# Delta rule: the small merge matmuls of a head as single items of the planner, and its last merge in two batches of five chunks side by side

## The chip, the cores and the metric

The kernel runs on one core of one Trainium2 chip. The time is device microseconds of one execution. TensorE (PE in the profile; PEld is its weight load), VectorE (DVE), ScalarE (ACT), GpSimd (POOL) and SyncE (SP) each work through their own instructions in order, and wait for one another through semaphores. Transfers are issued by SyncE, some by ScalarE.

## What is computed

One layer over 1024 latent and 256 context tokens of width 1024. Branch A is a gated delta rule in two directions, 8 heads of 128 by 128; branch B is a differential attention. The part that matters here, cut from the reference:

```python
    decay = jnp.where(incl, jnp.exp(jnp.where(incl, gc[..., :, None] - gc[..., None, :], 0.0)), 0.0)
    a_mat = jnp.where(strict, jnp.einsum('nbhid,nbhjd->nbhij', kc * bc[..., None], kc) * decay, 0.0)
    eye = jnp.eye(CHUNK, dtype=a_mat.dtype)
    t_mat = lax.linalg.triangular_solve(eye + a_mat, jnp.broadcast_to(eye, a_mat.shape),
                                        left_side=True, lower=True)
    u = t_mat @ (vc * bc[..., None])
    w = t_mat @ (kc * (bc * jnp.exp(gc))[..., None])
...
        v_new = u_i - jnp.einsum('bhck,bhkv->bhcv', w_i, s)
        s_next = s * jnp.exp(gl_i)[..., None, None] + jnp.einsum('bhck,bhcv->bhkv', kd_i, v_new)
```

`t_mat` is the inverse of a lower triangular matrix for every head, direction and chunk. The kernel takes chunks of 128 tokens, ten of them (NT): eight of the latents and two of the context.

## The kernel before

**Preparing a head (`gdn_prep`, from L972).** For each head, X holds ten chunks times two directions of 128x128. It is filled with the broadcast sums of the gates (gcd, on SyncE, L980), turned into decay factors on ScalarE (L997, L999), and multiplied with the Gram matrices (gram) that TensorE makes. The 32x32 diagonal blocks go through memory to VectorE, which inverts them in 31 steps (tmp, ts, L1048 and L1050). They come back as RR (R and its transpose Rt), and TensorE merges them:

- first merge, 32x32: pz = (block below the diagonal) x (inverse); VectorE negates it into Z (L1071); p2 = inverse x Z is the missing 32x32 block, p3 the same in the transposed order for t64. Forty pz, forty p2 and twenty p3 matmuls for a head (4, 4 and 2 for a chunk). ScalarE and VectorE copy them to X (L1087, L1089) and t64.
- last merge, 64x64: pz6 and Z6 (L1110), then pu6, two matmuls for a chunk in each. GpSimd clears a quarter of X (L1119), ScalarE copies pu6 into X (L1121, L1122), scales X by beta (L1126), and SyncE stores it to xd (L1129). This is done for chunks 5 to 9, and then for chunks 0 to 4.

In the profile pz and pz6 are both "pz", p2 and p3 are "p", pu6 is "pu"; they stand at L55, the helper `mm`. The 32x32 and 64x64 matmuls use quarters and halves of TensorE's array, several beside each other.

**The scan (`scan`, L1183; `out_chunk`).** Two streams, one for each direction, go through the ten chunks of a head: three chained 128x128 float32 matmuls (chain) with VectorE (r, S) and ScalarE (vd, vn) between, and two more for the output (out). It reads X back from xd (x, L1176) and keys, values and queries (sk, kk, vv, sq, L1161).

**The fill.** Input projections that nothing else here needs (mm, 128x512, operands of 128x128) are used as fill: they may go wherever TensorE has a hole.

**What sets the order.** All of this stage is written in an order that a planner (`flow`, `step`) makes when the program is built. Each piece of work is a generator, and each `yield` is one item: the engine, its assumed time, the items that it waits for, the code to emit, and for some TensorE items the share of the array that they keep warm. At every step the planner takes the item that can start first, with a bias for each stream (scan 0, preparation 3) and the fill last. The engines' real order is then fixed. One small matmul was one item of 0.03 us (32x32) or 0.065 us (64x64), so items of other streams could be placed between two of them.

**PSUM.** Merges, gram, the output transposes (oT) and the key transposes (tr) share two buffers (`self.banks`, `yield self.psum(n)` waits for n of them). pz takes one, p2 and p3 take two, and pz6 and pu6 took one each.

A head's X buffer is used again two heads later: the reload X<-gcd waits until both stores to xd have landed.

After the stage comes the attention (S, t, v), ordered by the same planner with other rules (`turn_flow`), the merge of the branches, and the output projection.

Of the kernel before, what the change touches and what calls it, by code (L numbers as in the profile page):

```python
# [23 lines left out]
NT = LT // P  # L24
# [10 lines left out]
PE, DVE, ACT, POOL, DMA, ADMA, DV2, PL1 = range(8)  # L35
# [8 lines left out]
class Block:  # L44
# [8 lines left out]

    def mm(self, out, lhsT, rhs, start=True, stop=True):
        self.nc.tensor.matmul(out, lhsT, rhs, start=start, stop=stop)  # L55

    def tr(self, out, src):
        self.nc.tensor.transpose(out, src, self.ident[:src.shape[0], :src.shape[0]])  # L58
# [913 lines left out]
    def gdn_prep(self, h):  # L972
        nc, PT, V = self.nc, self.gt_, self.nc.vector
        T = lambda nm, shape, tag=None: self.g1.tile(shape, F32, tag=tag or nm, name=nm)
        G = lambda nm, shape: self.gh[h % 2].tile(shape, F32, tag=nm, name=nm)
        X = G("X", [P, 2, NT, P])
# [18 lines left out]
        for d in range(2):  # L995
            for c in range(NT):
                t = yield ACT, 0.293, [ld[d]], lambda: nc.scalar.activation(  # L997
                    X[:, d, c], X[:, d, c], AF.Abs, bias=self.gcc[:, c, d * H + h:d * H + h + 1], scale=-1.0)
# [31 lines left out]
        B = lambda b: slice(32 * b, 32 * b + 32)  # L1030
# [66 lines left out]

        lo, hi = slice(0, 64), slice(64, 128)
        Z6 = T("Z6", [P, NT, 64], "w4")
        ends = []  # L1100
        for c0, nb in ((5, 5), (0, 5)):
            cs = slice(c0, c0 + nb)
            yield self.psum()
            b = self.banks.pop(0)
            pz = PT("pz6")[:, :nb * 64].rearrange("p (c f) -> p c f", f=64)
            for j in range(nb):
                c = c0 + j
                t = yield PE, 0.065, [tx, b], lambda: self.mm(pz[lo, j], X[hi, 0, c, lo], X[hi, 0, c, hi]), 0.5
                t = yield PE, 0.065, [tx, b], lambda: self.mm(pz[hi, j], X[lo, 1, c, hi], X[lo, 1, c, lo]), 0.5
            tz = yield DVE, 0.398, [t], lambda: V.tensor_scalar_mul(Z6[:, cs], pz, -1.0)  # L1110
            self.banks.append(tz)
            yield self.psum()
            b = self.banks.pop(0)
            pu = PT("pu6")[:, :nb * 64].rearrange("p (c f) -> p c f", f=64)
            for j in range(nb):
                c = c0 + j
                t = yield PE, 0.065, [tz, t6, b], lambda: self.mm(pu[lo, j], t64[lo, c], Z6[lo, c]), 0.5
                t = yield PE, 0.065, [tz, t6, b], lambda: self.mm(pu[hi, j], t64[hi, c], Z6[hi, c]), 0.5
            e = [(yield PL1, 0.38, [tz], lambda: nc.gpsimd.memset(X[hi, 0, cs, lo], 0.0)),  # L1119
                 (yield PL1, 0.38, [tz], lambda: nc.gpsimd.memset(X[lo, 1, cs, hi], 0.0))]  # L1120
            f = [(yield ACT, 0.43, [t], lambda: nc.scalar.copy(X[lo, 0, cs, hi], pu[lo])),  # L1121
                 (yield ACT, 0.43, [t], lambda: nc.scalar.copy(X[hi, 1, cs, lo], pu[hi]))]  # L1122
            self.banks.append(f)
            for d in range(2):
                for c in range(c0, c0 + nb):
                    t = yield ACT, 0.263, [e, f], lambda: nc.scalar.activation(  # L1126
                        X[:, d, c], X[:, d, c], AF.Copy, scale=self.beta[:, c, d * H + h:d * H + h + 1])
                ends.append(t)
            self.store_t.setdefault(h, []).append((yield DMA, 2.2, ends, lambda: nc.sync.dma_start(  # L1129
                self.xd[h][:, :, cs], X[:, :, cs])))  # L1130
        self.merge = self.stored = h + 1
# [732 lines left out]
```

## Time and profile before

| | us |
|---|---|
| median of 3 runs | 2091.38 |
| lowest and highest | 2090.12, 2092.27 |
| span of the profiled execution (first to last instruction) | 2084.9 |
| first and last merge matmul (pz of head 0, pu of head 7) | 632.2, 1303.1 |
| first and last scan matmul (chain) | 803.9, 1366.1 |
| TensorE busy, 600 to 1400 us | 778.7 of 800 |

For the profiled execution the profile gives the span, which leaves out what lies before the first and after the last instruction; the median is 6.5 us longer. In the rows of the timeline a start, a length, the engine, the line, the operation and the tiles follow each other; xN is the number of records. Matmuls overlap in the array, so the distance from one start to the next is what a matmul costs, and the length is not.

### The profile page before, as it was taken

To read this page: it belongs to the slowest core of one execution; us is meant where nothing else is said; L and a number is where in the kernel's file an instruction comes from. 1 tells how busy PE (TensorE), PEld (TensorE's weight loads), DVE (VectorE), ACT (ScalarE), POOL (GpSimd) and SP (SyncE) were. 2 spreads that over 40 slices of the span, in tenths; PEclk is the share of its full clock that TensorE was granted. 3 is DMA by queue.
4 is the path that set the end of the run, shared out by engine and by line. 5 is a ranking of instruction groups with operands and counts; after the bars stand their busy time and mean duration, and the time that the engine had idled before them with its cause. 6 is when DMAs were issued, how large, how long until landed. Compare 5 with 4: busy or idle time off the path is not lost.

```text
span 2084.9 us, 38611 instructions
## 1 busy us (share of the span) xinstructions
PE 1985.0 (95%) x14207; PEld 1733.2 (83%) x14207; DVE 1424.1 (68%) x3582; ACT 1070.7 (51%) x2328; POOL 774.7 (37%) x644
## 2 busy tenths in 40 slices
PE   8999898899999999999999999999899999999999
PEld 3888677789999997888778888887777878887899
DVE  4897668867876895657646885237767979874532
ACT  4344344444235453566456655448667878873210
POOL 1213224204441431323333232326555656764122
PEclk9999999999999999999999999999999999998999
DMA  9446567555446456656765763857465655236452
GB/s 310 124 139 152 150 143 190 139 166 172 138 136 214 134 200 174 222 179 207 195 214 151 252 199 109 252 161 213 115 175 134 174 158 148 87 126 207 149 157 90
DMA packets 395840, 352.24 MB, mean 169 GB/s; under 512 B 145423, under 2 KB 344689, under 8 KB 395651
## 3 DMA queue, kind: packets, MB, share of 16 engines
q1 hardware_dynamic: 345443, 302.58, 49.4%
q10 hardware_dynamic: 50208, 47.19, 7.5%
q8 instruction: 112, 1.84, 0.4%
q14 instruction: 77, 0.63, 0.1%
HBM read 232.63 MB, written 117.08 MB: 168 GB/s over the span
## 4 chain that ended last, share of the span: by engine, by line
PE 54%; DMA 9%; DVE 7%; ACT 4%; issue 2%; SPq 1%; POOL 1%; ACTq 0%; DVEq 0%; POOLq 0%
PE mm L55 22%; PE chain L55 5%; PE s L55 4%; PE mo L55 4%; PE v L55 4%; PE m L55 3%; PE ma L55 3%; PE out L55 3%; DVE S L1453 2%; PE t L58 2%; DMA wq<-in_w_oa_dram 2%; ACT S L1466 1%; DMA hx<-in_w_in_dram 1%; DMA qh<-qd 1%; PE gram L55 1%
## 5 line engine op out<-in xcount | busy, mean ns | idle before, releaser
L55 PE MATMUL mm<-hs,wh 128*128 128x512 f32 x1024 | 358.1, 414 | 0.0
L414 PE MATMUL mm<-hs,wh 128*128 128x512 f32 (+1 forms) x1024 | 291.5, 371 | 18.4 <-ACT xc L454 18.4
L55 PE MATMUL mm<-wh,hs 128*128 128x256 f32 x1472 | 273.3, 285 | 0.0
L1453 DVE TENSOR_SCALAR_CACHE_REDUCE S<-s,rsq 128x512 f32<-128x512 f32 (+1 forms) x384 | 242.4, 656 | 30.6 <-PE s L55 28.2
L414 PEld LDWEIGHTS mm<-hs,wh 128*128 128x128 f32 x1024 | 187.9, 194 | 52.5 <-ACT xc L454 21.7
L55 PEld LDWEIGHTS mm<-wh,hs 128*128 128x128 f32 x1472 | 230.9, 192 | 0.4
L1490 POOL TENSOR_TENSOR S<-S 128x1280 f32<-128x1280 f32 x64 | 188.9, 2954 | 100.0 <-ACT S L1483 91.1
L55 PE MATMUL mm<-hs,wl 128*128 128x512 f32 x512 | 213.7, 417 | 1.0 <-POOL wl L766 1.0
L55 PEld LDWEIGHTS mm<-hs,wh 128*128 128x128 f32 x1024 | 189.3, 191 | 27.1
L55 PE MATMUL mm<-wl,hs 128*128 128x256 f32 x736 | 210.3, 286 | 0.0
L1466 ACT ACTIVATE S<-S,mn 128x1280 f32<-128x1280 f32 x128 | 174.7, 1366 | 36.0 <-DVE mn L1465 35.5
L414 PE MATMUL mm<-hs,wl 128*128 128x512 f32 (+1 forms) x512 | 189.0, 369 | 0.0
L459 DVE SCALAR_TENSOR_TENSOR ac<-xc,smallT,ac 128x1284 f32<-128x1284 f32 (+1 forms) x96 | 159.0, 1656 | 14.2 <-ACT ac L455 11.9
L55 PE MATMUL s<-kk,qh 128*128 128x512 f32 (+1 forms) x384 | 146.7, 383 | 7.5 <-DVE S L1453 7.3
L55 PEld LDWEIGHTS mm<-wl,hs 128*128 128x128 f32 x736 | 141.1, 192 | 0.3
L55 PE MATMUL s<-kk,ql 128*128 128x512 f32 (+1 forms) x384 | 136.1, 364 | 0.1
L1527 DVE TENSOR_TENSOR al<-t,ah 128x512 fp32r<-128x512 f32 (+1 forms) x192 | 107.7, 595 | 13.2 <-ACT ah L1522 12.8
L414 PEld LDWEIGHTS mm<-hs,wl 128*128 128x128 f32 x512 | 99.2, 194 | 15.3
L55 PEld LDWEIGHTS mm<-hs,wl 128*128 128x128 f32 x512 | 97.7, 191 | 14.4 <-POOL wl L766 1.1
L1522 ACT CAST ah<-t 128x512 fp32r<-128x512 f32 (+1 forms) x192 | 90.3, 515 | 25.5 <-PE t L58 24.0
L1048 DVE TENSOR_TENSOR tmp<-ab,ts 80x31 f32<-80x31 f32 (+15 forms) x248 | 97.6, 394 | 8.1 <-DMA ab<-da 2.7
L58 PE MATMUL t<-ct,S 128*128 128x128 f32 x640 | 97.4, 278 | 5.3 <-DVE al L1527 4.8
(291 smaller groups left out, 5048.1 us busy)
## 6 DMA issues: line engine op xcount, KB each, us to landing
hx<-in_w_in_dram ACTq DMA_DIRECT2D x64, 256.0 KB
wr<-in_w_in_dram SPq DMA_DIRECT2D x30, 512.0 KB
X<-gcd SPq DMA_DIRECT2D x16, 640.0 KB
kd<-col SPq DMA_DIRECT2D x40, 256.0 KB
xd<-X SPq DMA_DIRECT2D x16, 640.0 KB
x<-xd SPq DMA_DIRECT2D x80, 128.0 KB
kk<-kd SPq DMA_DIRECT2D x32, 320.0 KB
wr<-in_w_in_dram ACTq DMA_DIRECT2D x18, 512.0 KB
```

What stands on the lines that cost most here:

```text
L55: self.nc.tensor.matmul(out, lhsT, rhs, start=start, stop=stop)
L58: self.nc.tensor.transpose(out, src, self.ident[:src.shape[0], :src.shape[0]])
L414: nc.tensor.matmul(pt[:, :n], wt[:, k, cs], ht[:, k, o:o + n], start=i == 0, stop=i == 3 * KT - 1)
L459: nc.vector.scalar_tensor_tensor(ac[:, w], xc[:, o + j:o + j + wd // parts], self.convw(j, ct), ac[:, w], ALU.mult, ALU.add)
L1048: t = yield DV2, n * w / 960.0 + 0.08, [t, t1], lambda: V.tensor_tensor(tv, ab[:, j + 1:, j:j + 1].to_broadcast([80, n, w]), ts[:, j, :w]. ...
L1453: e = yield DVE, 0.675 if m == 512 else 0.408, [e, self.sfree[c].get(n - 4 + c)], lambda: self.nc.vector.tensor_scalar(x["S"][c][:, o:o + ...
L1466: x["x"].append((yield ACT, 1.36, [e], lambda: nc.scalar.activation(S, S, AF.Exp, bias=x["mn"][:, c:c + 1], scale=-1.0, accum_out=w["l0"][ ...
L1490: e = yield POOL, 2.9, [e], lambda: self.nc.gpsimd.tensor_tensor(S0, S0, S1, ALU.add)
L1522: e = yield ACT, 0.48 if nb == 4 else 0.27, [t, y["old", k]], lambda: self.nc.scalar.copy(y["ah", k][:, :, q], pv)
L1527: t = yield DVE, 0.603 if k < 2 else 0.322, [e, y["old", k]], lambda: self.nc.vector.tensor_tensor(y["al", k][:, :, q], pv, y["ah", k][:, ...
```

## The change

The 40 pz of a head are one item, so are its 40 p2, and its 20 p3, through the new helper `mms`, which emits a list of matmuls. In p2 and p3 the order was four p2, two p3 for each chunk in turn; now all p2 come ahead of all p3. The last merge takes both halves together: 20 pz6 in one item into two PSUM buffers, two negations, 20 pu6 in one item into two buffers, and then for each half what followed before (clear, copy, scale, store). The assumed time of an item is the sum or a little more: 1.2, 1.2, 0.4, 1.3 and 1.3 us.

```diff
+    def mms(self, ops):
+        for x in ops:
+            self.mm(*x)
...
-        for c in range(NT):
-            for (b1, b2) in ((0, 1), (2, 3)):
-                t = yield PE, 0.03, [tt, b], lambda: self.mm(pz[B(b1), c], X[B(b2), 0, c, B(b1)], Rt[B(b2), c]), 0.25
-                t = yield PE, 0.03, [tt, b], lambda: self.mm(pz[B(b2), c], X[B(b1), 1, c, B(b2)], R[B(b1), NT + c]), 0.25
+        t = yield PE, 1.2, [tt, b], lambda: self.mms(
+            x for c in range(NT) for b1, b2 in ((0, 1), (2, 3)) for x in (
+                (pz[B(b1), c], X[B(b2), 0, c, B(b1)], Rt[B(b2), c]), (pz[B(b2), c], X[B(b1), 1, c, B(b2)], R[B(b1), NT + c]))), 0.25
...
-        for c in range(NT):
-            for (b1, b2) in ((0, 1), (2, 3)):
-                t = yield PE, 0.03, [tz, b], lambda: self.mm(p2[B(b1), c], R[B(b1), c], Z[B(b1), c]), 0.25
-                t = yield PE, 0.03, [tz, b], lambda: self.mm(p2[B(b2), c], Rt[B(b2), NT + c], Z[B(b2), c]), 0.25
-            t3 = yield PE, 0.02, [tz, b], lambda: self.mm(p3[B(1), c], Z[B(0), c], R[B(0), c]), 0.25
-            t3 = yield PE, 0.02, [tz, b], lambda: self.mm(p3[B(2), c], Z[B(3), c], Rt[B(3), NT + c]), 0.25
+        t = yield PE, 1.2, [tz, b], lambda: self.mms(
+            x for c in range(NT) for b1, b2 in ((0, 1), (2, 3)) for x in (
+                (p2[B(b1), c], R[B(b1), c], Z[B(b1), c]), (p2[B(b2), c], Rt[B(b2), NT + c], Z[B(b2), c]))), 0.25
+        t3 = yield PE, 0.4, [tz, b], lambda: self.mms(
+            x for c in range(NT) for x in ((p3[B(1), c], Z[B(0), c], R[B(0), c]), (p3[B(2), c], Z[B(3), c], Rt[B(3), NT + c]))), 0.25
...
-        for c0, nb in ((5, 5), (0, 5)):
-            cs = slice(c0, c0 + nb)
-            yield self.psum()
-            b = self.banks.pop(0)
-            pz = PT("pz6")[:, :nb * 64].rearrange("p (c f) -> p c f", f=64)
-            for j in range(nb):
-                c = c0 + j
-                t = yield PE, 0.065, [tx, b], lambda: self.mm(pz[lo, j], X[hi, 0, c, lo], X[hi, 0, c, hi]), 0.5
-                t = yield PE, 0.065, [tx, b], lambda: self.mm(pz[hi, j], X[lo, 1, c, hi], X[lo, 1, c, lo]), 0.5
-            tz = yield DVE, 0.398, [t], lambda: V.tensor_scalar_mul(Z6[:, cs], pz, -1.0)
-            self.banks.append(tz)
-            yield self.psum()
-            b = self.banks.pop(0)
...
-                t = yield PE, 0.065, [tz, t6, b], lambda: self.mm(pu[lo, j], t64[lo, c], Z6[lo, c]), 0.5
-                t = yield PE, 0.065, [tz, t6, b], lambda: self.mm(pu[hi, j], t64[hi, c], Z6[hi, c]), 0.5
...
+        halves = slice(5, 10), slice(0, 5)
+        v6 = lambda nm: PT(nm)[:, :5 * 64].rearrange("p (c f) -> p c f", f=64)
+        yield self.psum(2)
+        b = [self.banks.pop(0), self.banks.pop(0)]
+        pz = [v6("pz6"), v6("pz6")]
+        t = yield PE, 1.3, [tx, b], lambda: self.mms(
+            x for cs, z in zip(halves, pz) for j in range(5) for c in (cs.start + j,) for x in (
+                (z[lo, j], X[hi, 0, c, lo], X[hi, 0, c, hi]), (z[hi, j], X[lo, 1, c, hi], X[lo, 1, c, lo]))), 0.5
+        tz = []
+        for cs, z in zip(halves, pz):
+            tz += [(yield DVE, 0.398, [t], lambda: V.tensor_scalar_mul(Z6[:, cs], z, -1.0))]
+            self.banks.append(tz[-1])
+        yield self.psum(2)
+        b = [self.banks.pop(0), self.banks.pop(0)]
+        pu = [v6("pu6"), v6("pu6")]
+        t = yield PE, 1.3, [tz, t6, b], lambda: self.mms(
+            x for cs, u in zip(halves, pu) for j in range(5) for c in (cs.start + j,) for x in (
+                (u[lo, j], t64[lo, c], Z6[lo, c]), (u[hi, j], t64[hi, c], Z6[hi, c]))), 0.5
+        for cs, u in zip(halves, pu):
...
```

More of the change, by code (lines that the diff above doesn't have):

```diff
@@ L1099, in gdn_prep @@
         Z6 = T("Z6", [P, NT, 64], "w4")
-        ends = []
-        for c0, nb in ((5, 5), (0, 5)):
-            cs = slice(c0, c0 + nb)
-            yield self.psum()
-            b = self.banks.pop(0)
-            pz = PT("pz6")[:, :nb * 64].rearrange("p (c f) -> p c f", f=64)
-            for j in range(nb):
-                c = c0 + j
-                t = yield PE, 0.065, [tx, b], lambda: self.mm(pz[lo, j], X[hi, 0, c, lo], X[hi, 0, c, hi]), 0.5
-                t = yield PE, 0.065, [tx, b], lambda: self.mm(pz[hi, j], X[lo, 1, c, hi], X[lo, 1, c, lo]), 0.5
-            tz = yield DVE, 0.398, [t], lambda: V.tensor_scalar_mul(Z6[:, cs], pz, -1.0)
-            self.banks.append(tz)
-            yield self.psum()
-            b = self.banks.pop(0)
-            pu = PT("pu6")[:, :nb * 64].rearrange("p (c f) -> p c f", f=64)
-            for j in range(nb):
-                c = c0 + j
-                t = yield PE, 0.065, [tz, t6, b], lambda: self.mm(pu[lo, j], t64[lo, c], Z6[lo, c]), 0.5
-                t = yield PE, 0.065, [tz, t6, b], lambda: self.mm(pu[hi, j], t64[hi, c], Z6[hi, c]), 0.5
[L1119 to L1122, printed above, removed]
@@ L1123, in gdn_prep @@
+        for cs, u in zip(halves, pu):
+            e = [(yield PL1, 0.38, tz, lambda: nc.gpsimd.memset(X[hi, 0, cs, lo], 0.0)),
+                 (yield PL1, 0.38, tz, lambda: nc.gpsimd.memset(X[lo, 1, cs, hi], 0.0))]
+            f = [(yield ACT, 0.43, [t], lambda: nc.scalar.copy(X[lo, 0, cs, hi], u[lo])),
+                 (yield ACT, 0.43, [t], lambda: nc.scalar.copy(X[hi, 1, cs, lo], u[hi]))]
             self.banks.append(f)
+            ends = []
             for d in range(2):
-                for c in range(c0, c0 + nb):
-                    t = yield ACT, 0.263, [e, f], lambda: nc.scalar.activation(
+                for c in range(cs.start, cs.stop):
+                    t1 = yield ACT, 0.263, [e, f], lambda: nc.scalar.activation(
```

2 lines of the change are left out of this document (1 added, 1 removed).

## The prediction

> **What bounds the kernel now.** I read the page first (span, busy shares, the 40 slices, the shares of the chain), then busy time by stage, then TensorE's waits, then the timeline at single merges.
>
> ```profile
> span 2084.9 us, 38611 instructions
> ...
> PE 1985.0 (95%) x14207; PEld 1733.2 (83%) x14207; DVE 1424.1 (68%) x3582; ACT 1070.7 (51%) x2328; POOL 774.7 (37%) x644
> ...
> PE 54%; DMA 9%; DVE 7%; ACT 4%; issue 2%; SPq 1%; POOL 1%; ACTq 0%; DVEq 0%; POOLq 0%
> ```
>
> TensorE is busy for 95% of the span, and it has 54% of the chain that ended last. The merges lie between 632 and 1303 us. By stages (busy time of each engine, granted clock, DMA share and rate):
>
> ```profile
> 600.00:800.00 200.00, 198.57 (x2061) 192.71 (x2061) 159.21 (x417) 90.26 (x205) 55.76 (x47) 1.00 0.59 185
> 800.00:1000.00 200.00, 191.23 (x1603) 162.57 (x1602) 125.99 (x381) 118.43 (x352) 62.09 (x87) 0.98 0.63 197
> 1000.00:1200.00 200.00, 189.87 (x1549) 160.74 (x1548) 127.10 (x360) 115.74 (x316) 62.20 (x78) 0.97 0.65 200
> 1200.00:1400.00 200.00, 198.99 (x1594) 169.30 (x1593) 97.73 (x260) 99.05 (x292) 63.87 (x83) 1.00 0.59 177
> ```
>
> In these 800 us TensorE is idle for 1.4 + 8.8 + 10.1 + 1.0 = 21.3 us only; no other engine reaches 80% in any of the four. The projection matmuls (mm) fill every hole that the scan leaves. They still have work when the scan is over: the chain, in order of time, holds this piece after the last scan step at 1366 us:
>
> ```profile
> 1367.73 13.41 PE mm L55 x59
> ```
>
> So the end of this stage is set by the sum of what TensorE does plus its waits. Its waits here (total, times, longest):
>
> ```profile
> PE chain L55 <- ACT vd L1214: 7.9, 3, 4.7
> PE chain L55 <- DMA x<-xd: 2.9, 1, 2.9
> PE oT L58 <- POOL oa L1283: 2.6, 1, 2.6
> PE chain L55 <- DMA hx<-in_w_in_dram: 2.0, 1, 2.0
> ```
>
> None of them is on a merge. A merge is worth something here only through TensorE's own time, or through waits that it makes elsewhere.
>
> **The change part by part.** (1) *Units.* The planner now places each merge step as one item, so no other matmul can come between its small ones. How often did that happen? I counted, in the instruction order of the two programs, unbroken runs of 32x32 and of 64x64 matmuls on TensorE. Before: 62 runs of 32x32 and 49 of 64x64. After: 21 and 16. The number of small matmuls is the same (800 and 320), as is that of all others. So 41 + 33 = 74 breaks go, 58 of which are due to the units and 16 to the joined halves of the last merge. Heads 0 and 1 had no broken 32x32 run before; the breaks are in heads 2 to 7, where the scan runs beside the merges.
>
> What is a break worth? The timeline has a whole run (start, length, x records; a float32 matmul leaves two records):
>
> ```profile
> 631.96 0.28 PE L55 MATMUL mm<-wh,hs 128*128 128x256 f32 x1
> 632.17 0.89 PE L55 MATMUL pz<-RR,X 32*32 32x32 f32 x80
> 632.98 0.39 PE L55 MATMUL mm<-wh,hs 128*128 128x256 f32 x1
> ```
>
> And a broken one, followed by a place where the same kind of scan matmul stands among its like:
>
> ```profile
> 827.37 0.52 PE L55 MATMUL pz<-RR,X 32*32 32x32 f32 x36
> 827.82 0.49 PE L55 MATMUL out<-S,sq 128*128 128x128 f32 x2
> 828.24 0.25 PE L55 MATMUL pz<-RR,X 32*32 32x32 f32 x4
> 828.42 0.49 PE L55 MATMUL chain<-r,x 128*128 128x128 f32 x2
> ...
> 837.17 0.39 PE L55 MATMUL chain<-vd,kk 128*128 128x128 f32 x2
> 837.39 0.39 PE L55 MATMUL out<-vn,qk 128*128 128x128 f32 x2
> ```
>
> From start to next start (lengths overlap, so they can't be added): 36 records take 827.82 - 827.37 = 0.45 us, 4 records take 0.18. That is 0.0084 a record and a fixed 0.146 for each run. The whole run of 80 agrees: 0.146 + 80 x 0.0084 = 0.82, against 0.81 measured. The scan matmul between two runs takes 0.42, against 0.22 in a row of its like: 0.20 more. A 32x32 break therefore costs 0.146 + 0.20 = **0.35 us**. For 64x64:
>
> ```profile
> 848.91 0.57 PE L55 MATMUL pu<-Z,t 64*64 64x64 f32 x12
> 849.40 0.49 PE L55 MATMUL out<-S,sq 128*128 128x128 f32 x2
> 849.82 0.45 PE L55 MATMUL pu<-Z,t 64*64 64x64 f32 x8
> 850.20 0.50 PE L55 MATMUL mm<-hs,wl 128*128 128x512 f32 x1
> ```
>
> 12 records take 0.49, 8 take 0.38: 0.0275 a record and 0.16 fixed; with the 0.20 of the matmul between them (0.42 again), **0.36 us**. The sum: 41 x 0.35 + 33 x 0.36 = 14.4 + 11.9 = **26.2 us** of TensorE time. Nothing hides it, since the engine has next to no idle time there; it is lost only if TensorE then waits.
>
> (2) *The order inside p2 and p3.* Forty p2 then twenty p3 instead of four and two by turns: the same records in the same array form, at nothing; bounds 0 and one fixed 0.35 a head where other work falls between the two units (five heads; already in the count of runs).
>
> (3) *The last merge in two batches.* Both halves' pz6 in one go of 40 records (0.16 + 40 x 0.0275 = 1.3 us), then two DVE scalings, then both pu6. It needs both PSUM buffers at once, twice a head; before it needed one at a time. Who else wants them (gram, oT, tr) is put elsewhere in the fixed order, so this shows as waits, not as work. The scan's matmuls, which could slip in before, stand behind up to 1.3 us of small matmuls; the fills cover that as they covered the rest.
>
> (4) *The stores.* Still two a head, but in SyncE's order they now stand side by side for heads 4 to 6, and for heads 4 and 5 the reload X<-gcd comes right behind, ahead of sk, kk and vv of the next scan; before, for head 4, these stood between the stores. This is the dangerous part. Before, at head 4 (second store, reload, ScalarE's first use of it, and the scan matmul that waited for ScalarE):
>
> ```profile
> 1066.57 0.53 SPq L1129 DMA_DIRECT2D xd<-X  x1
> ...
> 1073.18 0.85 SPq L980 DMA_DIRECT2D X<-gcd  x2
> ```
>
> ```profile
> 1085.64 3.04 ACT L997 ACTIVATE X<-X,gcc 128x128 f32<-128x128 f32 x10 [5.96 <-DMA qk<-qkd]
> ...
> 1089.21 1.28 ACT L999 ACT_TABLE_LOAD   x1
> ```
>
> ```profile
> 1093.99 1.22 PE L55 MATMUL chain<-vd,kk 128*128 128x128 f32 x4 [4.69 <-ACT vd L1214]
> ```
>
> The reload was issued 6.6 us after the store and used 12.5 us later; ScalarE works in order, so vd of the scan stood behind it, and TensorE stood still for 4.7 us. Then the clock fell, as it did after other waits:
>
> ```profile
> 1002.00:1006.00 4.00, 1.99 (x12) 1.43 (x11) 0.05 (x1) 1.10 (x3) 1.63 (x1) 1.00 1.07 356
> 1006.00:1010.00 4.00, 4.00 (x17) 3.37 (x15) 0.58 (x2) 1.15 (x3) 0.00 (x0) 0.57 0.69 141
> ...
> 1091.00:1098.00 7.00, 4.01 (x25) 3.19 (x25) 1.79 (x5) 6.12 (x14) 2.17 (x3) 0.53 0.01 2
> ```
>
> A wait of 2.0 us cost a further 4 x 0.43 = 1.7 us at half clock; that of 4.7 us a further 7 x 0.47 = 3.3 us, 8.0 in all.
>
> The Trainium skill ("TensorE: Matmul & The Clock Gate", the table under "Why this matters for your kernels") asks for no idle gaps over about 3 us, since one idle window takes the clock to half. Here the measurement is stricter: 2.0 us was enough. By the page's limit the two waits that I add below would cost 3.4 us less, for a sum of -18.7.
>
> (5) *ScalarE.* Its order holds two more activation table loads than before, at 1.28 us: 2.6 us. At 51% busy they may cost nothing; the upper end is that both fall ahead of a vd, 2.6. I take 2.6, as vd is the longest wait above.
>
> (6) *Everything behind.* The planner's clocks change, so the order of all engines differs until deep in the attention stage (some 1,400 of 4,000 TensorE places moved); the work is the same. Its cost is unknown in sign: no row of before shows it. I bound it by one wait of the largest kind, 8.0 us either way, and take 0.
>
> What TensorE saves, it partly returns by arriving early. From nothing to all 26.2; I take two waits of the sizes that this stage shows for late transfers (2.9 and 2.0), each with 1.7 us of half clock: 8.3 us.
>
> Sum: -26.2 + 8.3 + 2.6 = **-15.3 us**. The profiled span of 2084.9 becomes 2069.6. The median of the runs, 2091.4, lies 6.5 above the span; carried over, **2076 us**.
>
> **The rivals.** *All of it arrives* (22%): 26.2 us, 2084.9 - 26.2 + 6.5 = 2065. For it: TensorE is 97% busy in the stage, and fills are left after the scan. Against: the 21.3 us of idle show that the fixed order is often a few us off.
>
> *The waits eat it* (15%): three waits like that at 1094, 24.0 us, leave 2.2: 2089. For it: DMA runs at 177 to 200 GB/s in the stage, and the stores come in pairs now.
>
> *Slower by the reload* (10%): SyncE stands at X<-gcd until the second of two stores has landed, and the next scan's loads stand behind it. The issues of 600 to 1400 us hold it for six heads, two each:
>
> ```profile
> X<-gcd SPq DMA_DIRECT2D x12, 640.0 KB
> ```
>
> If each head gives a wait of 8.0 us where one did, 5 x 8.0 = 40.0 are added: 2084.9 - 26.2 + 40.0 + 6.5 = 2105. It decides from four new waits on (26.2 / 8.0 = 3.3). Against: heads 2, 3 and 7 keep other issues between, and the planner starts the scan later where it expects the loads late.
>
> *The clock* (2%): long runs of small matmuls leave most of the array empty. If each of the 16 stretches of merges brought 1.7 us of half clock, 27 us would go: 2092. Against it, the whole 32x32 runs of head 0 before:
>
> ```profile
> 632.00:637.00 5.00, 4.61 (x220) 4.16 (x219) 4.66 (x14) 0.42 (x1) 1.50 (x4) 1.00 0.02 3
> ```
>
> The clock there is 1.00. *Doing nothing* isn't open: the runs are shorter in number in the program itself.
>
> **How the numbers follow.** Forecast 45%, and 6% for an attention order that is worse or better by more than 8 us. Less than 0.2%, 4.2 us, can't be told from no change. The forecast, the full gain, half of the eaten one and some of the rest are faster: 0.78; within 0.2%: 0.11; slower: 0.11. The range goes from the full gain with one wait of 3.7 less (2062) to the eaten case (2090); beyond lie the reload and the clock above, and two lucky waits below.
>
> **What would show it.** Right: 37 runs of small matmuls in the timeline, each with about 0.15 us fixed, and the stretch from the first merge to the last projection matmul shorter by about the sum. Returned waits: idle in 600 to 1400 over 21 us, with chain as the waiter and vd, x<-xd or X<-gcd as the cause. Reload: waits of 4 to 5 us at several heads, with clock rows near 0.5 behind them. Wrong would be: a merge stage no shorter though the runs are whole and the idle time is the same (then a break costs no 0.35), or a gain lost behind 1400 us, in the attention's waits.

## The result, and the profile after

The changed kernel takes **2106.9 us** (median of 4 runs, 2105.5 to 2108.3), the kernel before beside it 2090.8 (4 runs, 2089.7 to 2092.3). The ratio is **1.0075, interval 1.0061 to 1.0089**: 16 us slower, where 15 us faster was forecast. The time lies outside the range.

From the page of the changed kernel, the span and the busy times:

```profile
span 2106.0 us, 38576 instructions
...
PE 1972.6 (94%) x14207; PEld 1731.6 (82%) x14207; DVE 1416.7 (67%) x3582; ACT 1072.3 (51%) x2330; POOL 777.1 (37%) x644
```

TensorE is busy for 1972.6 us against 1985.0, 12 us less, and the span is 21 us longer all the same. So there are some 33 us more of idle time. By stages of the changed kernel (the same columns as before: busy time of PE, PEld, DVE, ACT, POOL, then clock, DMA share, GB/s):

```profile
600.00:800.00 200.00, 194.28 (x2057) 190.06 (x2056) 157.56 (x398) 90.43 (x207) 56.92 (x48) 1.00 0.55 173
800.00:1000.00 200.00, 191.67 (x1618) 166.26 (x1616) 122.97 (x373) 118.49 (x334) 60.85 (x82) 0.98 0.64 202
1000.00:1200.00 200.00, 181.94 (x1597) 155.97 (x1597) 127.51 (x375) 115.98 (x324) 61.00 (x80) 0.95 0.66 204
1200.00:1400.00 200.00, 192.81 (x1534) 167.91 (x1533) 99.55 (x271) 98.50 (x304) 68.45 (x87) 0.98 0.55 171
1400.00:1900.00 500.00, 459.89 (x2870) 398.11 (x2870) 384.79 (x1301) 362.26 (x598) 295.81 (x146) 0.96 0.55 148
```

And the last of these stretches, mostly attention, in the kernel before:

```profile
1400.00:1900.00 500.00, 470.26 (x2926) 406.63 (x2925) 390.54 (x1301) 365.50 (x604) 305.01 (x154) 0.97 0.55 154
```

From 600 to 1400 us TensorE is now idle for 5.7 + 8.3 + 18.1 + 7.2 = 39.3 us, before for 21.3. From 1400 to 1900 it is idle for 40.1, before for 29.7. The waits of TensorE from 600 to 1420 us in the changed kernel (total, times, longest):

```profile
PE oT L62 <- POOL oa L1286: 12.3, 3, 6.5
PE chain L55 <- DMA vv<-gv: 10.8, 4, 5.2
PE tr L62 <- DVE fin L884: 3.1, 3, 1.4
PE chain L55 <- DMA x<-xd: 2.8, 2, 2.7
PE chain L55 <- ACT vd L1217: 2.7, 3, 2.1
...
PE tr L62 <- DVE Z L1112: 1.4, 1, 1.4
...
PE pu L55 <- DVE Z L1112: 1.0, 1, 1.0
```

And the row for vv in the kernel before:

```profile
PE chain L55 <- DMA vv<-gv: 0.7, 1, 0.7
```

The wait for vd, the longest before, has shrunk from 7.9 to 2.7. Two others took its place: the output transposes wait for GpSimd (2.6 became 12.3), and the start of a scan waits for vv (0.7 became 10.8). The merges themselves have little of it: pu and the key transposes (tr) wait 1.0 and 1.4 us for the negation into Z6.

**Where the 16 us are.** I cut every profile at the same instructions: first pz, first and last score matmul (s) of attention. Up to the first pz TensorE's order is the same in both kernels, and the times (632.2 and 635.2 us) differ only as two executions do: the profiles of this study have 632.2 to 636.6 there. From the first pz (counted from the start of the matmul ahead of it) to the first s the changed kernel takes 4.9 us more (769.4 for 764.5), from the first to the last s 12.5 more (472.1 for 459.6), and behind that 0.7 more (229.6 for 228.9).

The first of these stretches holds the merges. To split it I took, in the kernel before, the median distance from one matmul's start to the next for each pair of kinds. Added up over a kernel's matmuls, with the time inside the small runs as it was, this is TensorE's *work*. What a distance has beyond the median is a *wait* where the row shows idle time, *half clock* where the clock is at half, and else *rest*. The table has the kernels that matter below too (time: median; ratio: to the kernel before in the same series, whose medians were 2090 to 2093):

| kernel | time, us | ratio | first pz to first s | work | waits | half clock | rest | first to last s |
|---|---|---|---|---|---|---|---|---|
| before | | 1 | 764.5 | 703.5 | 23.3 | 7.2 | 30.4 | 459.6 |
| changed | 2106.9 | 1.0075 | 769.4 | 679.7 | 43.2 | 13.0 | 33.6 | 472.1 |
| same_order | 2085.8 | 0.9950 | 755.0 | 681.9 | 28.7 | 7.4 | 37.0 | 463.1 |
| nudge_z | 2104.0 | 1.0074 | 767.2 | 703.3 | 26.4 | 7.0 | 30.5 | 471.0 |
| nudge_chain | 2132.4 | 1.0180 | 795.0 | 713.3 | 42.4 | 10.3 | 29.0 | 466.9 |
| nudge_chain2 | 2118.3 | 1.0121 | 778.0 | 713.2 | 24.7 | 9.8 | 30.3 | 476.3 |
| after_chain | 2120.0 | 1.0132 | 786.9 | 687.6 | 50.5 | 16.0 | 32.7 | 465.6 |
| after_chain2 | 2097.6 | 1.0029 | 758.0 | 685.6 | 30.5 | 7.3 | 34.6 | 468.7 |
| after_z | 2083.9 | 0.9967 | 753.2 | 679.0 | 35.5 | 4.0 | 34.7 | 463.0 |

The change takes 703.5 - 679.7 = 23.8 us of work away, and puts 19.9 us of waits, 5.8 of half clock and 3.2 of rest in its place.

Two limits of the table. Each row is one profiled execution, and executions of one and the same order differ: before and before_att_after (below) have one order up to attention, and take 764.5 and 770.1 us to the first s; mend_memset and mend_scale (below) 760.0 and 765.7. So the 4.9 us are not clear of chance. And where work ends and rest begins depends on how finely the kinds are told apart: with kinds by shape alone, the work falls by 16.3 us in the changed kernel and by 15.2 in same_order, for 23.8 and 21.6 in the table. Work and rest together don't depend on it. They fall by 20.6 and 15.0 us.

The matmuls themselves look as foreseen. From the timeline of the changed kernel, the 40 pz of a head in one piece beside a running scan:

```profile
1197.16 0.89 PE L55 MATMUL pz<-RR,X 32*32 32x32 f32 x80
1197.98 0.71 PE L55 MATMUL chain<-r,x 128*128 128x128 f32 x4
```

80 records take 0.82 us, as the 0.146 + 80 x 0.0084 of the prediction have it.

### The profile page after: what moved, and what is told of

The parts are those of the page before. It is cut to its first block, busy times and chain, and to the rows that moved or that the text cites. A ratio compares the mean times of both kernels' runs of the same rounds, so it can differ in the third digit from the quotient of the medians.

```text
span 2106.0 us, 38576 instructions
## 1 busy us (share of the span) xinstructions
PE 1972.6 (94%) x14207; PEld 1731.6 (82%) x14207; DVE 1416.7 (67%) x3582; ACT 1072.3 (51%) x2330; POOL 777.1 (37%) x644
## 5 line engine op out<-in xcount | busy, mean ns | idle before, releaser
L55 PE MATMUL mm<-hs,wh 128*128 128x512 f32 x1024 | 362.7, 419 | 0.0
L1530 DVE TENSOR_TENSOR al<-t,ah 128x512 fp32r<-128x512 f32 (+1 forms) x192 | 107.5, 594 | 19.9 <-ACT ah L1525 19.2
```

Of the source, the lines that this page charges most:

```text
L1530: t = yield DVE, 0.603 if k < 2 else 0.322, [e, y["old", k]], lambda: self.nc.vector.tensor_tensor(y["al", k][:, :, q], pv, y["ah", k][:, ...
```

## The experiments

**Theory:** a break costs what it was said to cost, and the loss comes from the order: the planner wrote a new one for every engine from the first head's merge on, and a new order has other waits. **Rivals:** the joined units themselves lose (they hold PSUM buffers, ScalarE or the stores at the wrong time); the two batches of the last merge lose; the reload behind paired stores loses.

### 1. The joining without the new order, and the parts

*same_order*: the kernel before; the small matmuls of a merge step are all emitted by the first of its items, and the other items stay in the planner and emit nothing. So the order of everything else stays as before, except in the last phase of the kernel (behind attention), where some transfers and matmuls change places. 48 runs of small matmuls instead of 111.

```diff
+    def once(self, ops):
+        for x in ops:
+            self.mm(*x)
+        ops.clear()
...
-                t = yield PE, 0.03, [tt, b], lambda: self.mm(pz[B(b1), c], X[B(b2), 0, c, B(b1)], Rt[B(b2), c]), 0.25
-                t = yield PE, 0.03, [tt, b], lambda: self.mm(pz[B(b2), c], X[B(b1), 1, c, B(b2)], R[B(b1), NT + c]), 0.25
+        for _ in range(4 * NT):
+            t = yield PE, 0.03, [tt, b], lambda: self.once(ops), 0.25
```

> The planner still sees one item per small matmul, so the order of everything else is that of before, up to the last phase; but the first item of a merge step emits the whole step, and the others emit nothing. The last merge stays in two halves. Runs of small matmuls: 48 instead of 111. Theory A (a break costs 0.35 us of TensorE, and the new order, not the joining, gave it back): 63 x 0.35 = 22 us less work; with some returned waits 12 to 22 us faster than before, 2069 to 2079 us. Theory B (joined runs hold up the scan and make the waits themselves): no gain or slower, 2088 to 2105 us. Theory C (a break costs next to nothing): within 4 us of before.

Measured: 0.9950 of the kernel before (0.9928 to 0.9972), **some 10 us faster** (6 by the medians). The median of 2085.8 us lies above the range of Theory A and below those of the two others. By the table, 63 breaks less take 703.5 - 681.9 = 21.6 us of work away, 0.34 each. 12 of them come back as waits (5.4) and rest (6.6). Counted with the rest, a break is worth 15.0 / 63 = 0.24 us here, and 20.6 / 74 = 0.28 in the changed kernel; 0.35 is the upper end. In the last phase, whose order did change, this kernel takes 236.7 us from the last s to the end against 228.9. The joining doesn't account for these 8 us, and part of them may be chance: the changed kernel and mend_memset have one order there and take 229.6 and 234.5.

*after_att_before* and *before_att_after*: the changed kernel with attention in the order that it had before, and the kernel before with attention in the order that it has in the changed one. The planner's choice is replaced by a list.

```diff
-            self.step(min((x for x in heads if x[1] == eng and x[0] <= first + self.TOL), key=lambda x: (x[2][1] or 0.0, x[0]))[2])
+            s = self.streams[ord(ATT[self.placed_]) - 48]
...
+            self.step(s)
```

> The changed kernel up to the end of the scan stage, with the order of the attention stage replayed item by item as before had it. The profile of the changed kernel has 12.4 us more between the first and the last score matmul than before. Theory A1 (the attention order that the planner made from other clocks costs this): 10 to 13 us faster than the changed kernel, 2094 to 2097 us. Rival A2 (the attention loses because it starts from another state of transfers and buffers, whatever its order): no change, 2104 to 2109 us.

> The reverse: the kernel before up to the end of the scan stage, with the attention order of the changed kernel replayed. Theory A1 (the order costs): 10 to 13 us slower than before, 2101 to 2104 us. Rival A2 (the state at its start): within 4 us of before, 2087 to 2095 us.

Measured: 2099.0 us, 1.0025 (1.0003 to 1.0048), and 2104.7, 1.0066 (1.0038 to 1.0095). The new attention order costs the kernel before, in which no merge was touched, 13 us. Giving the old one back to the changed kernel brings it from 1.0075 to 1.0025. So some two thirds of the loss (0.0050 of 0.0075, uncertain by 0.0027) is in a stage that the change doesn't touch. 2099.0 lies between the ranges of A1 and A2. The profile of after_att_before, taken from one of its slowest executions (2106.8 us; they go from 2090.3 to 2108.0), doesn't show the gain: 470.4 us from the first to the last s, for 472.1 in the changed kernel. In the four profiles with TensorE's attention order of before (before, same_order, mend_both_att, after_att_before) this stretch takes 459.6, 463.1, 463.7 and 470.4 us, in the five with that of the changed kernel and no edit in attention (changed, mend_memset, mend_reload, mend_reload7, before_att_after) 470.4 to 472.3.

*units_only*: the changed kernel with the last merge in two separate halves, as before, each a unit (54 runs).

```diff
-        yield self.psum(2)
-        b = [self.banks.pop(0), self.banks.pop(0)]
-        pz = [v6("pz6"), v6("pz6")]
...
+        for c0, nb in ((5, 5), (0, 5)):
...
+            t = yield PE, 0.65, [tx, b], lambda: self.mms(x for j in range(nb) for c in (c0 + j,) for x in (
```

> Half of the change: each merge step is one item of the planner, but the last merge is still done half after half, with one buffer at a time and the two stores apart. Runs: 54 instead of 111, 57 x 0.35 = 20 us less TensorE time. If both halves side by side (two buffers at once, stores in pairs ahead of the reload) make the waits of the merge stage: 10 to 20 us faster than before, 2071 to 2081 us. If any new order gives back what the units save: within 15 us of before on either side, 2085 to 2105 us, with waits at places of its own.

Measured: 2111.5 us, 1.0079 (1.0049 to 1.0108). This is above both ranges, and no better than with the two batches, so these are not needed for the loss. In its profile the loss stands in attention: 758.4 us from the first pz to the first s, and 486.0 from there to the last s, where it has 55 more records of matmuls than before, so that part of this is moved work.

*two_batch*: the other half alone: two batches, but single items as before (104 runs).

```diff
-        t = yield PE, 1.3, [tx, b], lambda: self.mms(
-            x for cs, z in zip(halves, pz) for j in range(5) for c in (cs.start + j,) for x in (
...
+        for cs, z in zip(halves, pz):
+            for j in range(5):
+                c = cs.start + j
+                t = yield PE, 0.065, [tx, b], lambda: self.mm(z[lo, j], X[hi, 0, c, lo], X[hi, 0, c, hi]), 0.5
```

> The kernel before with the second half of the change alone: the last merge takes all ten chunks in two batches, its matmuls still single items of the planner (104 runs of small matmuls for 111, a new order). Theory (a new order loses by itself, and 7 runs less give 2.5 us): 2095 to 2130 us. Rival (the two batches alone are harmless or a gain, and the joined units lose): 2083 to 2092.

Measured: 2122.4 us, 1.0159 (1.0136 to 1.0183). Each half of the change alone is at least as slow as both together. Costs that belong to the parts would add up; these don't, which is what one expects if every version simply has an order of its own. The two batches do have a small cost of their own: in all 12 profiles of kernels with them, pu waits 0.5 to 1.1 us for Z near 647 us, and tr 1.4 us for Z near 711 us (the rows above); in the 7 others neither row stands.

### 2. A new order with no change at all

Three kernels in which the planner is given one other number, and nothing else. *nudge_z*: the assumed time of the negation into Z. *nudge_chain*: that of one 128x128 float32 matmul of the scan's chain (r with x), one thousandth of a microsecond up. *nudge_chain2*: that of all of them (chain, out and gram, seven places), one thousandth down.

```diff
-        tz = yield DVE, 0.398, [t], lambda: V.tensor_scalar_mul(Z, pz, -1.0)
+        tz = yield DVE, 0.41, [t], lambda: V.tensor_scalar_mul(Z, pz, -1.0)
```

```diff
-                t = yield PE, 0.2235, [tr, u["tx"]], lambda: self.mm(pc[:, 1], u["x"][:, c % 2], r)
+                t = yield PE, 0.2245, [tr, u["tx"]], lambda: self.mm(pc[:, 1], u["x"][:, c % 2], r)
```

> The kernel before with one other number changed in the planner alone, the due cost of the eviction of Z from 0.398 to 0.41 us: no unit is joined, the work is the same, the order comes out new from the first merge on (107 runs of small matmuls for 111). Theory (a new order loses by itself): 2095 to 2135 us, the size by chance. Rival (the first altered number happened on a bad order, a new order is as good as the old on the average): 2080 to 2100.

> The kernel before with one number changed in the planner alone, the due cost of a scan's chain matmul from 0.2235 to 0.2245 us: no unit is joined, the work is the same, but the planner's order comes out new from the first scan on (102 runs of small matmuls for 111). Theory (a new order loses by itself, whatever made it, because the order shown was one with few waits): 2095 to 2115 us, 5 to 25 above the kernel before, with TensorE's waits of 5 us and more at new places. Rival (the loss comes from the units: their length, or their banks held longer): 2087 to 2094, as before.

> The kernel before with the cost of a 128-wide fp32 matmul at 0.2225 us for 0.2235 (111 runs, new order). Theory (a new order without joined units loses against the one shown): 2095 to 2135. Rival (a new order is as good as the old on the average): 2080 to 2100.

Measured: 1.0074 (1.0054 to 1.0094), 1.0180 (1.0155 to 1.0204) and 1.0121 (1.0094 to 1.0149). **A kernel in which nothing is changed but one number of the planner, by 3%, loses as much as the changed one**, and the two others lose 38 and 25 us (2132 is more than the 2095 to 2115 expected of nudge_chain). Two stretches of nudge_z, then of nudge_chain, by the columns above:

```profile
600.00:1400.00 800.00, 776.11 (x6803) 684.18 (x6802) 505.06 (x1410) 425.55 (x1168) 244.94 (x296) 0.99 0.61 188
1400.00:1900.00 500.00, 462.35 (x2868) 399.90 (x2867) 384.91 (x1301) 360.44 (x596) 295.78 (x146) 0.95 0.54 148
```

```profile
600.00:1400.00 800.00, 757.75 (x6708) 670.50 (x6707) 502.90 (x1405) 417.44 (x1140) 239.09 (x288) 0.98 0.60 185
1400.00:1900.00 500.00, 469.83 (x2875) 401.73 (x2874) 381.38 (x1292) 356.67 (x606) 292.45 (x146) 0.97 0.54 145
```

nudge_z loses nothing in the merge stage (776.1 busy of 800, before 778.7) and 8 us of TensorE's busy time from 1400 to 1900; nudge_chain has 42.3 us idle in the merge stage for 21.3. Its work is 10 us more as well, as 39 more records of other matmuls stand ahead of its first s. The same two losses, in other shares, make up the changed kernel's.

In attention it is even the same order: from the first to the last s, TensorE's 2,741 records follow each other in nudge_z exactly as in the changed kernel, and the stretch takes 471.0 and 472.1 us. So the changed kernel's loss there is one that the planner also makes with no change to the merges.

### 3. Other orders of the changed kernel

The same two kinds of number in the changed kernel: *after_chain* (0.2245) and *after_chain2* (0.2225), both in all seven places, and *after_z* (0.41), with 35, 35 and 37 runs of small matmuls. The diffs are of the kind shown above.

> The changed kernel with the planner's cost of a 128-wide fp32 matmul at 0.2245 us for 0.2235: the units stay joined (35 runs of small matmuls), the work is the same, the order comes out new. Theory (the time is that of a draw of orders, less 25 us of TensorE work for the joined runs): anywhere from 2080 to 2110, not the changed kernel's 2107 again. Rival (the joined units hold something that costs 15 us in any order): 2103 to 2115.

> The same with 0.2225 us for 0.2235 (35 runs). Theory: from 2080 to 2110, another value than the first. Rival: 2103 to 2115.

> The changed kernel with the planner's cost of the eviction of Z at 0.41 us for 0.398 (37 runs). Theory: from 2080 to 2110, another value again; the mean of the four orders with joined units, this one among them, lies some 25 us below the mean of the newly drawn orders without (2132 and 2104 so far). Rival: 2103 to 2115.

Measured: 1.0132 (1.0106 to 1.0158), 1.0029 (1.0012 to 1.0046) and **0.9967 (0.9949 to 0.9985)**. The same joined units take anything from 2084 to 2120 us, by the order. The rival, by which all three stay at 2103 to 2115, is out; after_chain, at 2120, is above the theory's range too. The mean of the four orders with joined units (changed, after_chain, after_chain2, after_z) is 1.0051, that of the three nudged ones without 1.0125: 0.0074 or 15 us between them. The single values lie so far apart (0.006 either side) that this is uncertain by some 10 us (one standard error); 24 us of work less a returned part fit it, and no difference can't be excluded. Nor are the draws independent: in attention, after_z alone of the newly planned kernels has the order of before, but for where some fills stand, and it is the fastest; nudge_chain2 and after_chain have one and the same attention order on TensorE.

### 4. Single waits of the new order

In these kernels every engine's order is a list, written as the planner made it, and only the places named are changed. The list stands at the top of the file, so a line has a higher number here than in the changed kernel.

*mend_memset.* From 1005 us on in the changed kernel, GpSimd's timeline, then the row of TensorE that waited, then SyncE's:

```profile
1016.96 1.27 POOL L770 TENSOR_TENSOR wl<-hx,wh 128x512 fp32r<-128x512 f32 x1 [8.16 <-ACT wh L769]
1023.88 0.95 POOL L1045 MEMSET ts<- 80x1024 f32 x1 [5.65 <-DMA db<-ts]
1024.79 1.64 POOL L176 TENSOR_TENSOR of<-of,mhalf 128x8 f32<-128x8 f32 x1
1026.39 0.15 POOL L1046 MEMSET ts<- 80x32 f32 x1
1026.51 1.90 POOL L1286 TENSOR_TENSOR oa<-oa,of 128x1024 f32<-128x1024 f32 x1
```

```profile
1028.46 1.12 PE L62 MATMUL oT<-ct,oa 128*128 128x128 f32 x4 [6.46 <-POOL oa L1286]
```

```profile
1008.16 5.11 SPq L1164 DMA_DIRECT2D sq<-gq  x1
1013.38 4.70 SPq L1038 DMA_DIRECT2D da<-X  x4
...
1019.91 1.29 SPq L1056 DMA_DIRECT2D db<-ts  x1
```

The memset of ts (the buffer of the next inversion) has no condition in the planner, but on the chip it waits until the store db<-ts has read the buffer. SyncE issued that store only at 1019.9, behind sq and da. GpSimd works in order, so the output norm (of, oa) stood behind the memset for 5.7 us, and TensorE's transposes behind the norm. The edit, in GpSimd's order:

```diff
-memset ts (L1045)
 of<-of,mhalf
-memset ts (L1046)
 oa<-oa,of
+memset ts (L1045)
+memset ts (L1046)
```

> The changed kernel with every engine's order written out as it is, but for one edit: for one head, the two memsets of ts stand behind one power and one scaling of oa on GpSimd instead of ahead of them, so that they no longer wait for the store of db in front of that output. Theory (single waits): TensorE's 6.5 us wait for oa at 1021 us goes, and with it up to 6.8 us lost at half clock: 2094 to 2101 us, 6 to 13 below the changed kernel's 2107. Rival (spread loss): 2105 to 2108.

Measured: 2101.8 us, 1.0041 (1.0022 to 1.0060), 5 us less. In its timeline the norm is ahead, and TensorE's wait is 2.3 us:

```profile
1017.83 1.65 POOL L288 TENSOR_TENSOR of<-of,mhalf 128x8 f32<-128x8 f32 x1 [1.56 <-DVE of L1395]
1019.56 1.89 POOL L1398 TENSOR_TENSOR oa<-oa,of 128x1024 f32<-128x1024 f32 x1
1021.94 0.95 POOL L1157 MEMSET ts<- 80x1024 f32 x1 [0.49 <-DMA db<-ts]
```

```profile
1021.51 1.12 PE L187 MATMUL oT<-ct,oa 128*128 128x128 f32 x4 [2.30 <-POOL oa L1398]
```

*mend_scale*: the same, and at the start of attention two scalings of S on ScalarE stand earlier. From the changed kernel, ScalarE's three scalings in a row, what GpSimd did behind them, and TensorE behind that:

```profile
1432.73 3.85 ACT L1486 ACTIVATE S<-S,rl 128x1280 f32<-128x1280 f32 x3
```

```profile
1434.15 8.64 POOL L1493 TENSOR_TENSOR S<-S 128x1280 f32<-128x1280 f32 x3 [13.95 <-ACT S L1486]
```

```profile
1437.10 2.18 PE L62 MATMUL t<-ct,S 128*128 128x128 f32 x9 [10.72 <-POOL S L1493]
```

GpSimd stood still for 14 us, as ScalarE did three exps, a zo eviction and three casts ahead of the first scaling. nudge_z has the same 10 us wait at the same matmul:

```profile
1432.41 2.18 PE L58 MATMUL t<-ct,S 128*128 128x128 f32 x9 [10.39 <-POOL S L1490]
```

```diff
 S<-S,mn (exp)
+S<-S,rl
 zo<-mm
 S<-S,mn (exp)
+S<-S,rl
 ah<-t x3
 S<-S,mn (exp)
-S<-S,rl x2
 S<-S,rl
```

> The changed kernel with every engine's order written out as it is, but for two edits: the two memsets of ts stand behind one power and one scaling of oa on GpSimd (measured alone: 2101.8 us), and two scalings of S on ScalarE at the start of attention stand three and four of its operations earlier, each right behind an exp and ahead of a zo eviction or casts. Theory (single waits add up): TensorE's 10.6 us wait for GpSimd's S at 1430 us shrinks to 3 or less, and part of the 10.2 us at half clock behind it goes: 2090 to 2096 us. Rival (a wait taken away comes back elsewhere): 2099 to 2104.

Measured: 2097.1 us, 1.0032 (1.0015 to 1.0048), between the two ranges, and not clear of mend_memset's 1.0041 (1.0022 to 1.0060). The wait is 3.7 us now, and stands for another cause:

```profile
1424.14 1.94 PE L187 MATMUL t<-ct,S 128*128 128x128 f32 x8 [3.71 <-DVE al L1642]
```

7 us of wait became 3.1 us less from the first to the last s (471.9 to 468.8).

*mend_reload* and *mend_reload7* go for the reload X<-gcd, which stands on SyncE ahead of the next scan's loads. The first moves it behind them at one head, the second at the next. The wait of 5.2 us for vv, at 1184.7 us, belongs to the second; the first, whose expectation speaks of that wait, was put one head too early.

```diff
-X<-gcd x2, kq<-gk, kq<-gq
 x<-xd, qk<-qkd (several)
 sk<-gk, kk<-gkk, vv<-gv, sq<-gq
+X<-gcd x2, kq<-gk, kq<-gq
```

> The changed kernel with every engine's order written out as it is, but for one edit: for one head, the two loads of X's correction planes and the two loads of kq stand behind the next scan's four loads (sk, kk, vv, sq) on SP instead of ahead of them. Theory (a handful of single waits, each made by the new order, holds the loss): the 5.2 us wait of TensorE for vv at 1179 us goes, and with it up to 3.4 us of half clock: 2098 to 2102 us, 5 to 9 below the changed kernel's 2107. Rival (the loss is spread, and a wait taken away comes back behind the next operand): 2105 to 2108.

> The changed kernel with every engine's order written out as it is, but for one edit, this time at the head whose scan waits 5.2 us for vv at 1184 us: its reload (two X, two kq) stands on SP behind the four loads of the next scan. Theory A (vv is late only because it stands behind the reload): that wait goes and nothing else comes: 2099 to 2103 us. Theory B (the eight loads want the DMA at the same time, and whichever stands last is late: ScalarE's multiplication of X, and zo queued behind it, wait for X in its place, as at the head before): 2106 to 2115.

Measured: 2115.0 us, 1.0107 (1.0083 to 1.0131), and 2105.9, 1.0082 (1.0063 to 1.0101). No gain. In the changed kernel (SyncE, then TensorE):

```profile
1160.93 0.84 SPq L984 DMA_DIRECT2D X<-gcd  x2
...
1172.87 0.37 SPq L1164 DMA_DIRECT2D vv<-gv  x1
```

```profile
1184.73 1.22 PE L55 MATMUL chain<-vv,x 128*128 128x128 f32 x4 [5.20 <-DMA vv<-gv]
```

In mend_reload7 (SyncE, ScalarE, TensorE):

```profile
1159.07 0.45 SPq L1276 DMA_DIRECT2D vv<-gv  x1
...
1163.57 0.90 SPq L1096 DMA_DIRECT2D X<-gcd  x2
```

```profile
1171.43 3.03 ACT L1113 ACTIVATE X<-X,gcc 128x128 f32<-128x128 f32 x10 [10.83 <-DMA X<-gcd]
```

```profile
1179.30 1.22 PE L180 MATMUL mm<-hs,wh 128*128 128x512 f32 x2 [9.17 <-ACT zo L1033]
```

The wait for vv is gone, and ScalarE waits 10.8 us for X instead; the eviction zo stands behind that in ScalarE's order, the PSUM buffer stays full, and TensorE stands still for 9.2 us. Here a wait did come back elsewhere, and larger. In mend_reload the same happened one head earlier (8.7 us for zo), and the 5.2 us for vv stayed (4.7).

*mend_both_att*: the first reload edit and the memset edit together, with attention in the order of before.

> The changed kernel with both edits, and with the attention in the order that it had before the change. Theory (single waits): 2099 as measured with that attention order alone, less 11 to 22 us: 2077 to 2088 us, below the kernel before. Rival (spread loss): 2096 to 2100.

Measured: 2101.2 us, 1.0036 (1.0019 to 1.0052), above both ranges and no better than with the attention order alone (2099.0). What the memset edit gave, the reload edit may have taken: TensorE's wait for zo, of 8.7 us, is there as in mend_reload.

*z_memset*: the memset edit in after_z, whose order is that of the changed kernel up to there.

> The fastest order of the joined units so far (Z's eviction at 0.41 us; 2084 us, 0.9967 of the kernel before), written out as it is, but for the one edit that helped the changed kernel: the two memsets of ts behind one power and one scaling of oa on GpSimd. Both orders are the same up to there, and TensorE waits there 7.4 us. Theory (one in-order queue, one wait): 5 to 8 us go, as they did in the changed kernel: 2076 to 2080 us. Rival (a wait taken away comes back elsewhere): 2082 to 2085.

Measured: 2084.4 us, 0.9951 (0.9932 to 0.9969). TensorE's wait there fell from 7.4 to 1.5 us, and the time not by a measurable amount. Counted from the first pz, this kernel was 5 us ahead of after_z at 1100 us, and 2 at the first s: a scan that starts earlier finds vv later (2.8 us for 1.9 at 1243). So the memset edit gave 5 us in one order and nothing certain in the other. The fastest versions, z_memset, same_order and after_z, take 0.995 to 0.997 of the kernel before, and can't be told from one another.

## Why the prediction was wrong

- **(1) Units: right in kind, the price at its upper end.** 74 breaks went, and the work fell by 23.8 us (21.6 us for 63 in same_order), against 26.2 worked out; with the rest counted in, by 20.6 (15.0), which is 0.28 (0.24) a break for 0.35.
- **(2) Order inside p2 and p3: right.** The time inside the small runs rose from 34.1 to 35.5 us, the work above having this in it.
- **(3) Two batches:** the cost came as waits, as the text said, but the fills did not cover it at two places: 1.0 us on pu and 1.4 on tr, which the sum has at nothing. It is small beside the loss; units_only, without them, is as slow.
- **(4) The reload:** the mechanism exists, at one head and with 5.2 us. The rival that built on it named 2105 us, close to what came, but by five more waits of 8.0 us, one a head. That the number is near is luck: there was one of 5.2 us, and moving the reload gains nothing.
- **(5) Table loads:** two more, as counted. The wait for vd, which they were to lengthen, fell from 7.9 to 2.7 us.
- **(6) "Everything behind" failed.** The text took the new order "at 0", bounded by "one wait of the largest kind, 8.0 us either way". Seven newly planned orders with and without joined units, and units_only and two_batch besides, lie from 0.9967 to 1.0180, a spread of 45 us; the three with nothing but a planner number changed all lie above 1, by 15, 25 and 38 us (0.0074, 0.0121 and 0.0180 of 2091). Taking the order as neutral was the mistake twice: the width was several times 8 us, and its middle was not 0, since the order shown is better than those that the planner gave with another number. In the profile of the changed kernel the new order took 28.9 us in the stretch with the merges (19.9 + 5.8 + 3.2) and 12.5 in attention, against 23.8 saved. The surest figure is that of attention: its new order alone made the kernel before 13 us slower (before_att_after).
- **The returned waits** (8.3 us) were taken as the whole answer of the merge stage. Where the order stays (same_order), waits and rest rise by 12 us, so that term was of the right kind and a little small; in the changed kernel waits and half clock rise by 25.7.
- **The clock:** this rival put 27 us on long runs of small matmuls. same_order has such runs too, and its half clock takes 7.4 us for 7.2.
- **Span to median:** 6.5 us before, 0.9 now; the spans differ by 21, the medians by 16. In every run that has both figures the time is 1.7 to 1.9 us above the span of its own execution. So the profiled execution of the kernel before took about 2086.7 us, 4.7 less than the median: of the 6.5 us, 4.7 were a quick execution, and the differences between the two profiles are some 5 us too large.

Of the marks that the prediction set, the idle time over 21 us in the merge stage and a "gain lost behind 1400 us, in the attention's waits" both came true. The causes named for the first did not: it is not vd, x<-xd or X<-gcd that grew, but GpSimd's oa and vv.

What stays open: why the order of before is better than the others, and how much of the 16 us is in the stretch with the merges, where the two profiles differ by no more than two executions of one order. That its numbers were chosen with its time in view would do it, but no run here shows that. Nor was it tried to give the planner the condition of the memset, which it lacks.

## What to carry to other kernels

Where a planner fixes the order of all engines, a change has two effects, and they are to be priced apart: what it saves, in the old order (emit the work differently and keep the items), and the draw of a new order, from a few kernels in which one planner number is nudged and nothing else. If nudges alone move the time by more than the saving, try several orders of the new version ahead of judging it. And look for what the planner doesn't know: a memory clear that waits for an old store, at the head of an in-order queue, held TensorE for 6.5 us.

## What the runs showed of the hardware

The half clock comes in fixed pieces. In the 19 profiles of this study there are 354 stretches with the clock at 0.5: 335 of them last 3.41, 6.83, 10.24, 13.65 or 20.48 us, multiples of 3.41, and the other 19, the last of each profile, are cut off by the end of the span. A stretch through which TensorE is busy costs half its length, so a wait costs either nothing more or at most 1.7 us, 3.4 and so on. Which of these is chance to a degree: the changed kernel and mend_memset have the same order up to 1017 us, and the same wait in both. First the row of TensorE and that of the 10 us around it in the changed kernel, then the same two in mend_memset:

```profile
878.07 0.71 PE L55 MATMUL chain<-vv,x 128*128 128x128 f32 x4 [2.08 <-DMA vv<-gv]
```

```profile
872.00:882.00 10.00, 7.92 (x43) 6.56 (x42) 1.86 (x9) 2.28 (x6) 4.83 (x3) 1.00 1.05 371
```

```profile
876.91 1.22 PE L180 MATMUL chain<-vv,x 128*128 128x128 f32 x4 [2.20 <-DMA vv<-gv]
```

```profile
872.00:882.00 10.00, 7.80 (x36) 6.54 (x36) 0.54 (x3) 2.16 (x5) 3.90 (x3) 0.83 1.04 386
```

2.1 us of waiting left the clock at 1.00 in one and brought it to 0.83 over the 10 us, one stretch of 3.4 us, in the other. The Trainium skill ("TensorE: Matmul & The Clock Gate", Part 1: The HAM clock gate) describes a free-running window of about 3.4 us in which activity is counted; the pieces of 3.41 us agree with it, and so does it that equal waits end differently, by where they fall in the window.
